# A third of the transposes of the normalised input, by the matrix engine in place of the DMA

## The chip, the cores and the metric

The kernel runs on one core of a Trainium2 chip. The metric is the device time of one execution in microseconds; the figure used is the median over several runs. The core's engines each run their own instruction stream in order: TensorE (PE, matrix products; its weight loads are shown apart as PEld), VectorE (DVE), ScalarE (ACT, called the activation engine in some places), GpSimd (POOL) and SyncE (SP), which in this kernel issues most of the DMA transfers. Streams wait for one another by semaphores.

## The reference, cut to what matters

A decoder block on x of 2048 rows by 1024 channels, in float32. Only the first stage concerns the change: x is normalised by row and multiplied by a wide input matrix; the first two blocks of columns of the product feed a recurrent branch, the rest feeds attention and gates.

```python
def rmsnorm(x, g):
    y = xf * lax.rsqrt(jnp.mean(xf * xf, axis=-1, keepdims=True) + NORM_EPS)
    return (y * g.astype(jnp.float32)).astype(x.dtype)
...
    u = rmsnorm(h, pre_g[l])
    z = jnp.einsum('bsd,df->bsf', u, w_in[l])
    xr, zr, q, k, v, za, gm = jnp.split(z, split_points, axis=-1)
    xc = causal_depthwise_conv(xr, conv_w[l], conv_b[l])
    y_r = rg_lru(xc, ...) * jax.nn.silu(zr)
...
    lam = exp(sum(attn_lq1 * attn_lk1)) - exp(sum(attn_lq2 * attn_lk2)) + lam_init
    o = diff_attention(qh, kh, vh, lam)
    m = g_r * (y_r @ w_br_rnn) + g_a * (y_a @ w_br_attn)
    h = h + rmsnorm(m @ w_out, post_g)
```

## The kernel before, in words

**The input.** x is taken in 16 tiles of 128 rows (tile i holds rows 128 i to 128 i + 127, 128 x 1024 float32). `load_x` has SP issue one transfer for a tile; five tiles are kept under way, and tile i + 5 is loaded when tile i is done with (L240). `x_stat` works on tiles in pairs: ACT squares a tile and sums each row (L256, `jk`), DVE turns the two sums into a row scale (`vx` at L257 and the small steps of an inverse square root behind it). `x_fin` then takes each tile: DVE multiplies it by the row scale and the channel gain (L266), ACT casts the product to fp16, the high half of `u16` (L269), and the rest, the low half, is the difference to that cast, made by DVE for even tiles and by POOL for odd ones (L270). Both halves are needed with channels on the partitions, so each is transposed into the tile `uT[p, hi/lo, k, s]`: channel k x 128 + p, row s. Before the change every one of these 32 transposes is a DMA that SP issues (L276):

```python
x_last[2] = la.ins
load_x(i + PD)
for hl_ in range(2):
    x_t[i] = nc.sync.dma_start_transpose(out=uT[:, hl_, :, i * 128:(i + 1) * 128],
                                         in_=u16[:, hl_])
```

**The weights.** The input matrix is used in blocks of 128 columns. A block is loaded (L145, `wst`), squared and summed by ACT (L156, `w_s` at L158), its total over the partitions taken by a 128 x 1 matmul into a PSUM tile called `tot` (L162), and it is split into a high and a low fp16 half by ACT (L177) and DVE (L178). `tot` comes from the pool `lpt`, which has two PSUM buffers.

**The first products.** A product of such a block with uT is three matmuls (high x high, high x low, low x high) for each of eight k, all at L192. The first three half rows (two `xr` blocks and a `zr` block, rows 0 to 1023) are not made one after another: their three PSUM tiles of 128 x 1024 stand open at once, and PE goes through x tiles 0 to 7, 72 matmuls of 128 x 128 for each, so that it can start on tile 0 while the later ones come. After that come the half rows of rows 1024 to 2047, in two chunks of 128 x 512 (24 matmuls each), then the further blocks.

**What follows on the other engines.** ACT reads an `xr` half row out of PSUM (L318); a four-tap convolution on POOL and DVE makes `xc`, which is split into two halves `xh` and `xl`; PE multiplies these by gate weights (L351 to L353) that DVE split before into `gwh` and `gwl` (L513, L514); ACT takes the tanh of the gates (L355, `th`). The four 64-element vectors of lambda come by DMA in `a_consts`; DVE takes two dot products (into `ld`, with `lj` as a tile for the products nobody reads), and ACT an exponential and a logarithm (L531 to L538).

**The order.** The kernel is written as one program, but the order in which it is written is not the order that runs: the framework reorders each engine's instructions at build by a simulated timeline (`TileContext(nc, schedule_with_timeline_sim=True)`). An edit in one place can therefore move instructions of other places on any engine. After the build, each engine's order is fixed.

Of the kernel before, what the change touches and what calls it, by code (L numbers as in the profile page):

```python
# [9 lines left out]
F32 = mybir.dt.float32  # L10
F32R = mybir.dt.float32r
F16 = mybir.dt.float16
# [3 lines left out]
ALU = mybir.AluOpType  # L16
# [11 lines left out]
EPS = 1e-6  # L28
GM_T = 8   # groups of gate projections kept for the end of the attention
LAG = 2    # units between a unit's scores and its product with v  # L30
ACC0 = 8.0  # projection groups ahead of the attention units
PD = 5     # x tiles loaded ahead
# order in an attention unit: scores (0, 1), exponentials (e), combination of the unit before (c),
# product with v of an earlier one (p), with projection groups between them (f: one, F: all that are due)
ORD = "0fc1eFp"
SEG_A = 2  # where a head's gate projections stand between its chunks
SEG_B = 5
# [11 lines left out]
def kernel(  # L49
# [44 lines left out]
    with ExitStack():  # L94
        ones = cst.tile([128, 128], F32, name="ones")
        nc.vector.memset(ones, 1.0)
        ones16 = cst.tile([128, 128], BF16, name="ones16")
        nc.vector.memset(ones16, 1.0)

        def tl(n, name):  # L100
# [27 lines left out]

# [1 line left out]
        class W:  # L130
            pass

        def w16_at(i):
            """one of the four places for a block of weights"""
            return lambda w: w16_p.tile([128, 2, KD, 128], F16, tag=f"w{i % 4}", name="w16")
# [24 lines left out]
        def w_scale(w, ps, fac, keep=None):  # L160
            """power of two that brings the block's norm close to 2^13 (a rough sum is enough for it)"""
            nc.tensor.matmul(ps[:, 0:1], ones16, w.ss, start=True, stop=True)  # L162
            tot = tl(1, "w_tot")
            nc.vector.tensor_scalar(out=tot, in0=ps[:, 0:1], scalar1=1e-30, scalar2=None, op0=ALU.max)
            w.sg, w.iv = keep or (tl(1, f"w_sg_{w.tag}"), tl(1, f"w_iv_{w.tag}"))
            pow2_bits(w.sg, tot, 13)
            pow2_inv(w.iv, w.sg)
            if keep is None:
                w.cz = wn_p.tile([128, 1], F32, tag=f"w_cz_{w.tag}", name="w_cz",
                                 bufs={"wg": 4, "agm": 3}.get(w.tag, 2))  # L170
                nc.vector.scalar_tensor_tensor(out=w.cz, in0=w.iv, scalar=fac, in1=cu, op0=ALU.mult, op1=ALU.mult)
# [9 lines left out]

# [1 line left out]
        utx = ExitStack()  # L183
# [3 lines left out]
        def mm3(ps, w, c0, n):  # L187
            """ps[f128, n] += w^T u over all of d, s in [c0, c0 + n)"""
            i = 0
            for k in range(KD):  # L190
                for a, b in ((0, 0), (0, 1), (1, 0)):
                    nc.tensor.matmul(ps, w.t[:, a, k, :], uT[:, b, k, c0:c0 + n],  # L192
                                     start=(i == 0), stop=(i == 3 * KD - 1))
                    i += 1

        # ================= RG-LRU branch =================
        with ExitStack() as lx:
# [21 lines left out]
            def prep_g(gr):  # L219
                """power of two that keeps the scaled, normalised input in fp16's range"""  # L220
                ss, tot = tl(1, "g_ss"), tl(1, "w_tot")
                jk = le.tile([KD, 128], F32, tag="idt", bufs=1, name="jg")
                nc.scalar.activation(jk, gr, AF.Square, accum_out=ss[0:KD])
                ps = lpt.tile([128, 1], F32, tag="tot", name="tot")
                nc.tensor.matmul(ps[:, 0:1], ones[0:KD, :], ss[0:KD], start=True, stop=True)
                nc.vector.tensor_scalar(out=tot, in0=ps[:, 0:1], scalar1=1e-30, scalar2=None, op0=ALU.max)
                pow2_bits(gi, tot, 10)
                pow2_inv(cu, gi)
# [34 lines left out]
            def x_fin(i0, n, gb):  # L263
                for i in range(i0, i0 + n):
# [10 lines left out]
                    for hl_ in range(2):  # L275
                        x_t[i] = nc.sync.dma_start_transpose(out=uT[:, hl_, :, i * 128:(i + 1) * 128],  # L276
                                                             in_=u16[:, hl_]).ins

            # weight pipeline
            order = [(C_XR if i % 2 == 0 else C_ZR) + (i // 2) * 128 for i in range(2 * KD)]  # L280
# [16 lines left out]
            def in_half(b, hf, z, w):  # L297
                """PSUM tile of a half row of an x_r (z = 0) or z_r (z = 1) block"""
                if hf == 0 and 2 * b + z < 3:
# [142 lines left out]
            x_fin(4, 2, gb)  # L442
            # per-channel vectors: rows of 128 channels, turned into columns
            rows = le.tile([65, 128], F32, tag="rows", bufs=1, name="rows")
# [24 lines left out]
            with tc.issue_after(x_last[1]):  # L469
                # block-diagonal gate weights, exact f32r hi/lo  # L470
                gf_t = []
# [13 lines left out]
            with after_x():  # L485
                nc.vector.tensor_scalar(out=ba, in0=ba, scalar1=0.5, scalar2=None, op0=ALU.mult)
                nc.vector.tensor_scalar(out=bx, in0=bx, scalar1=0.5, scalar2=None, op0=ALU.mult)
                # softplus(-a) = max(-a, 0) + log1p(exp(-|a|)), log1p(t) = 2 atanh(t / (2 + t))
                spm, spe, sps, spq, spr = (lc.tile([128, KD], F32, name=f"sp{i}") for i in range(5))
# [27 lines left out]
            def a_consts():  # L517
                with after_x():
# [7 lines left out]
                    ld = cst.tile([128, 2], F32, name="ld")  # L526
                    lj = cst.tile([128, 64], F32, name="lj")
                    for i in range(2):
                        nc.vector.tensor_tensor_reduce(out=lj, in0=lv[:, 2 * i, :], in1=lv[:, 2 * i + 1, :], op0=ALU.mult,
                                                       op1=ALU.add, scale=1.0, scalar=0.0, accum_out=ld[:, i:i + 1])  # L530
# [44 lines left out]

        # ================= differential attention and merge gates =================
        QT = S // 128
        wfac_a = cst.tile([128, KD], F32, name="wfac_a")
        ya_ss = cst.tile([128, NH * NC], F32, name="ya_ss")
        with ExitStack() as ax:  # L580
# [14 lines left out]

# [1 line left out]
            wl = {k: ws[2 * KD + i] for i, k in enumerate(ahead)}  # L597
# [16 lines left out]
            def wadv(n):  # L614
                """weight blocks up to index n ready; two more on their way"""
                while wpos[0] < min(n + 3, len(worder)) or wpos[1] < min(n + 2, len(worder)) or wpos[2] < min(n + 1, len(worder)):
# [38 lines left out]

# [1 line left out]
            Kt, Qt, Vt, Gt = {}, {}, {}, {}  # L657
# [133 lines left out]

# [1 line left out]
            class U:  # L793
# [179 lines left out]

        # ================= branch projections, merge, output projection =================
        with ExitStack() as bx_:
# [178 lines left out]

            # norm of the attention branch's rows, for a bound on the merged sum
            ya_n = bs.tile([128, 1], F32, name="ya_n")
# [52 lines left out]
```

## Time and profile before

| what | value |
|---|---|
| runs | 2505.09, 2502.2, 2505.01 us; median 2505.01 |
| profiled execution | 2506.1 us from its first to its last instruction, 1.1 above the median |
| PE busy | 2353.1 us, 94% |
| DVE busy | 1548.4 us, 62% |
| ACT busy | 1224.6 us, 49% |
| POOL busy | 679.7 us, 27% |
| DMA | 268.73 MB, 107 GB/s in the mean |

The profile is of one execution, in microseconds from the start of its span; the span is its own time. Line numbers (L192) are those of the kernel before. Names such as `ps<-uT,w` give the output and inputs of an instruction by the program's tiles. A number behind "x" is a count. Idle time is put down to the event that ended it, the releaser: "[6.43 <-ACT xr L318]" means that the engine stood still for 6.43 us, until ACT had done its instruction of line 318 that writes `xr`.

### The profile page before, as it was taken

Reading aid. Unit: us, or ns where it says so; the run is one execution under the profiler, and the core shown is the slowest. Engines: PE = TensorE matmul, PEld = TensorE weight load, DVE = VectorE, ACT = ScalarE, POOL = GpSimd, SP = SyncE. Lnnn points to the kernel's source line nnn. Section 1 sums busy time; section 2 is a strip of 40 time slices with the busy share of each in tenths; the row PEclk is TensorE's granted clock in tenths of the full one; section 3 lists DMA queues with packets and bytes.
Section 4 is the critical chain, followed back from the end, with each engine's and each line's share of the span. In section 5 each row is a group of like instructions: output and inputs, shape, how many; then the busy total and the mean of one; then the engine's idle time right before and its main releaser. Section 6 shows DMA issues by size and latency. Waiting matters only on the chain. (4 is left out here: it accounts for less than half of the span.)

```text
span 2506.1 us, 41430 instructions
## 1 busy us (share of the span) xinstructions
PE 2353.1 (94%) x15240; PEld 1355.3 (54%) x15240; DVE 1548.4 (62%) x4316; ACT 1224.6 (49%) x2156; POOL 679.7 (27%) x415
## 2 busy tenths in 40 slices
PE   6789999999998999998998999999999899999998
PEld 5344444465665665665665655655655444444443
DVE  8877667668658566667567478468467244633323
ACT  5555545456547546556456457356456244312211
POOL 3443334212222212222222222223123133322211
PEclk9899999999999999999999999999999999999999
DMA  9511111235444534635535445445445854743202
GB/s 244 104 43 48 46 42 34 76 81 119 108 96 111 113 84 108 127 82 113 115 84 114 103 96 118 95 90 124 95 90 115 251 177 135 239 148 118 84 17 101
DMA packets 541323, 268.73 MB, mean 107 GB/s; under 512 B 370504, under 2 KB 518016, under 8 KB 541120
## 3 DMA queue, kind: packets, MB, share of 16 engines
q1 hardware_dynamic: 538144, 256.74, 42.6%
q0 software_dynamic: 2816, 9.08, 1.2%
q8 instruction: 119, 1.95, 0.3%
q14 instruction: 84, 0.69, 0.1%
q10 hardware_dynamic: 160, 0.27, 0.0%
HBM read 110.79 MB, written 41.94 MB: 61 GB/s over the span
## 5 line engine op out<-in xcount | busy, mean ns | idle before, releaser
L192 PEld LDWEIGHTS <-w 128*128 128x128 f16 x5040 | 475.9, 100 | 576.5 <-issue 89.2
L192 PE MATMUL mm<-uT,w 128*128 128x512 f16 x3072 | 705.1, 383 | 12.9 <-ACT gm L728 8.9
L877 POOL TENSOR_TENSOR e<-e,e 128x1024 f16<-128x1024 f32 (+2 forms) x192 | 317.0, 1666 | 970.6 <-ACT e L876 487.0
L851 ACT ACTIVATE e<-e,nb,sc_h 128x1024 f32<-128x1024 f32 (+7 forms) x384 | 376.1, 980 | 160.8 <-DVE nb L845 125.6
L826 DVE TENSOR_SCALAR_CACHE_REDUCE e<-sc 128x1024 f32<-128x1024 f32 (+7 forms) x352 | 305.2, 880 | 134.9 <-PE sc L814 122.3
L192 PE MATMUL ps<-uT,w 128*128 128x512 f16 (+1 forms) x1968 | 354.4, 345 | 26.1 <-ACT xr L318 17.7
L711 PE MATMUL mm<-wva,uT 128*128 128x256 f16 x3072 | 352.7, 275 | 3.3 <-DVE st L668 2.6
L1094 PE MATMUL psb<-yt,w 128*128 128x512 f16 x1536 | 332.9, 379 | 2.0 <-ACT w L177 1.5
L711 PEld LDWEIGHTS <-uT 128*128 128x128 f16 x3072 | 301.5, 99 | 48.8 <-issue 2.9
L814 PE MATMUL sc<-K,Q 128*128 128x512 f16 (+3 forms) x1280 | 287.2, 351 | 19.9 <-DVE e L826 13.8
L897 PE MATMUL o<-V,pt 128*128 128x128 f16 x3264 | 224.5, 222 | 38.4 <-DMA pt<-e 38.1
L1094 PEld LDWEIGHTS <-w 128*128 128x128 f16 x1536 | 149.1, 98 | 184.9 <-issue 3.9
L897 PEld LDWEIGHTS <-pt 128*128 128x128 f16 x3264 | 200.0, 99 | 72.8 <-DMA pt<-e 46.5
L876 ACT ACTIVATE e<-e 128x1024 f16<-128x1024 f32 (+2 forms) x192 | 150.1, 802 | 143.1 <-DVE e L874 118.5
L814 PEld LDWEIGHTS <-Q 128*128 128x128 f16 x1280 | 119.6, 99 | 133.2 <-issue 20.2
L874 DVE SCALAR_TENSOR_TENSOR e<-e,rs,e 128x1024 f32<-128x1024 f32 (+2 forms) x192 | 190.0, 1017 | 2.2
L1125 PE MATMUL psf<-wo,m 128*128 128x512 f16 x720 | 155.7, 379 | 0.0
L156 ACT ACTIVATE jk<-wst 128x1024 bf16<-128x1024 f32 x80 | 84.2, 1052 | 138.7 <-DMA wst<-in_w_in_dram 102.6
L1125 PEld LDWEIGHTS <-m 128*128 128x128 f16 x768 | 75.1, 98 | 90.6
L1098 DVE SCALAR_TENSOR_TENSOR t<-gt,psb 128x512 f32<-128x512 f32 x64 | 43.8, 686 | 120.2 <-PE psb L1094 100.1
L1148 ACT ACTIVATE jk<-psf 128x1024 bf16<-128x1024 f32 x15 | 15.4, 1024 | 134.0 <-PE psf L1125 69.4
L717 DVE SCALAR_TENSOR_TENSOR V<-mm,V 128x256 f16<-128x256 f32 x64 | 26.9, 421 | 85.7 <-ACT V L716 85.6
(247 smaller groups left out, 2417.3 us busy)
## 6 DMA issues: line engine op xcount, KB each, us to landing
wst<-in_w_in_dram SPq DMA_DIRECT2D x64, 512.0 KB, 4.5
xt<-in_x_dram SPq DMA_DIRECT2D x32, 512.0 KB, 4.5
gm_d<-gm SPq DMA_DIRECT2D x64, 256.0 KB, 2.7
gt<-gm_d SPq DMA_DIRECT2D x32, 512.0 KB, 3.8
K<-st SPq DMA_DIRECT2D x128, 64.0 KB, 2.0
Q<-st SPq DMA_DIRECT2D x64, 128.0 KB, 2.4
Q<-st SPq DMA_DIRECT2D x128, 64.0 KB, 2.1
ya_d<-yT SPq DMA_DIRECT2D x64, 128.0 KB, 2.0
```

The source lines that it names most:

```text
L156: nc.scalar.activation(jk, w.st, AF.Square, accum_out=ss)
L192: nc.tensor.matmul(ps, w.t[:, a, k, :], uT[:, b, k, c0:c0 + n], start=(i == 0), stop=(i == 3 * KD - 1))
L711: nc.tensor.matmul(ps[:, j, :], uT[:, a, k, s0:s0 + 128], wt[:, b, k].rearrange("p t f -> p (t f)"), start=(i == 0), stop=(i == 3 * KD - 1))
L814: nc.tensor.matmul(ps[:, x * 128:x * 128 + m], Qt[h, t // 4][:, v, ci, q0:q0 + 128], K[:, ci, 0:m], start=(v == 0), stop=(v == 1))
L826: nc.vector.tensor_scalar(out=ev[:, 0:m], in0=ps[:, 0:m], scalar1=1.0, scalar2=None, op0=ALU.mult, op1=ALU.max, accum_out=u.mx[:, ci, col: ...
L851: nc.scalar.activation(ev[:, 0:nb * 128], ev[:, 0:nb * 128], AF.Exp, bias=nb_[:, ci:ci + 1], scale=sc_h[h], accum_out=u.sm[:, pi, ci:ci + 1])
L874: nc.vector.scalar_tensor_tensor(out=e0[:, 0:m], in0=e1v[:, 0:m], scalar=rs, in1=e0[:, 0:m], op0=ALU.mult, op1=ALU.add)
L876: nc.scalar.activation(e1[:, 0, 0:m], e0[:, 0:m], AF.Copy)
L877: nc.gpsimd.tensor_tensor(out=e1[:, 1, 0:m], in0=e0[:, 0:m], in1=e1[:, 0, 0:m], op=ALU.subtract)
L897: nc.tensor.matmul(o, pt[:, a, kb % 8, :], V[:, kb % 4, b, :], start=(kb == 0 and i == 0), stop=(kb == n - 1 and i == 2))
L1094: nc.tensor.matmul(ps, w.t[:, p, k, :], y_t[b][:, q, k, sl], start=(i == 0), stop=(i == 3 * KD - 1))
L1125: nc.tensor.matmul(pn[n], m16[:, a, j, ms], wo[:, b, j, ns], start=(j == 0 and a == 0 and b == 0), stop=(j == KD - 1 and a == 1))
```

## The change

For the x tiles with i % 3 == 2 (2, 5, 8, 11 and 14) a half is transposed by eight matmuls with an identity matrix `idh` into a PSUM tile `xps` (128 x 8 x 128 fp16), and ACT copies `xps` into uT. `xps` comes from `lpt` and shares the two buffers of the `tot` tiles. The other eleven tiles go by DMA as before. `idh` is built once at the start. To make room for it in SBUF the tile `lj` goes: the dot products of lambda now write their unread products over one of their own inputs. Line numbers of the changed kernel are 2 higher than before up to `x_fin`, and 7 or 8 higher behind it.

```diff
         ones16 = cst.tile([128, 128], BF16, name="ones16")
         nc.vector.memset(ones16, 1.0)
+        idh = cst.tile([128, 128], F16, name="idh")
+        make_identity(nc, idh)
...
                     load_x(i + PD)
                     for hl_ in range(2):
-                        x_t[i] = nc.sync.dma_start_transpose(out=uT[:, hl_, :, i * 128:(i + 1) * 128],
-                                                             in_=u16[:, hl_]).ins
+                        if i % 3 == 2:
+                            pt = lpt.tile([128, KD, 128], F16, tag="tot", name="xps")
+                            for k in range(KD):
+                                nc.tensor.transpose(pt[:, k, :], u16[:, hl_, k * 128:(k + 1) * 128], idh)
+                            nc.scalar.activation(uT[:, hl_, :, i * 128:(i + 1) * 128], pt, AF.Copy)
+                        else:
+                            x_t[i] = nc.sync.dma_start_transpose(out=uT[:, hl_, :, i * 128:(i + 1) * 128],
+                                                                 in_=u16[:, hl_]).ins
...
-                    lj = cst.tile([128, 64], F32, name="lj")
                     for i in range(2):
-                        nc.vector.tensor_tensor_reduce(out=lj, in0=lv[:, 2 * i, :], in1=lv[:, 2 * i + 1, :], op0=ALU.mult,
+                        nc.vector.tensor_tensor_reduce(out=lv[:, 2 * i, :], in0=lv[:, 2 * i, :], in1=lv[:, 2 * i + 1, :], op0=ALU.mult,
```

The reordering moves instructions beside those that the diff names. In the rows below, a row is an instruction in its engine's order: line, operation, output<-inputs with their shape; the number behind a tile's name tells its buffers apart and differs between the two builds.

The first place is SP's queue at the end of the loads of x. Before, `u16_419` is tile 9, `u16_484` tile 10 and `u16_492` tile 11; `xt_422` is the load of tile 14 and `xt_487` that of tile 15:

```order
L240 DMA xt_422<-in_x_dram 128x1024
L276 DMA_TRANSPOSE uT_82<-u16_419 128x8x128
L145 DMA wst_1231<-in_w_in_dram 128x8x128
L276 DMA_TRANSPOSE uT_82<-u16_484 128x8x128
L276 DMA_TRANSPOSE uT_82<-u16_492 128x8x128
L240 DMA xt_487<-in_x_dram 128x1024
L276 DMA_TRANSPOSE uT_82<-u16_484 128x8x128
L276 DMA_TRANSPOSE uT_82<-u16_492 128x8x128
```

Now `u16_478` is tile 9, `u16_543` tile 10, and `xt_455`, `xt_481` and `xt_546` are the loads of tiles 13, 14 and 15:

```order
L284 DMA_TRANSPOSE uT_87<-u16_478 128x8x128
L242 DMA xt_455<-in_x_dram 128x1024
L242 DMA xt_481<-in_x_dram 128x1024
L284 DMA_TRANSPOSE uT_87<-u16_478 128x8x128
L284 DMA_TRANSPOSE uT_87<-u16_543 128x8x128
L242 DMA xt_546<-in_x_dram 128x1024
L284 DMA_TRANSPOSE uT_87<-u16_543 128x8x128
L147 DMA wst_1326<-in_w_in_dram 128x8x128
```

The load of tile 15 stood behind both halves of tile 9, a weight block, and one half each of tiles 10 and 11; now it stands behind tile 9 and one half of tile 10, and the weight block comes after it.

The second place is ACT around the first read-out of `xr`. Before, `jk_535` is the square of tile 14 and `jk_537` that of tile 15; `xr_1193` is the first read-out, `u16_521` and `u16_527` are the casts of tiles 12 and 13:

```order
L269 ACTIVATE u16_484<-xt_330 128x1024
L269 ACTIVATE u16_492<-xt_373 128x1024
L256 ACTIVATE jk_535,ssx_532<-xt_422 128x1024
L318 ACTIVATE xr_1193<-ps_614,w_cz_180 128x1024
L386 ACTIVATE g_1209<-ps_615,w_cz_229 128x1024
L269 ACTIVATE u16_521<-xt_381 128x1024
L318 ACTIVATE xr_1212<-ps_616,w_cz_313 128x1024
L269 ACTIVATE u16_527<-xt_414 128x1024
L256 ACTIVATE jk_537,ssx_532<-xt_487 128x1024
```

Now `jk_612` and `jk_614` are the squares of tiles 14 and 15, `xps_554` and `xps_564` the two halves of tile 11, and `u16_598` is the cast of tile 12:

```order
L271 ACTIVATE u16_543<-xt_353 128x1024
L271 ACTIVATE u16_551<-xt_414 128x1024
L258 ACTIVATE jk_612,ssx_609<-xt_481 128x1024
L179 ACTIVATE w16_502<-wst_426,w_sg_wg_494 128x1024
L282 ACTIVATE uT_87<-xps_554 128x8x128
L258 ACTIVATE jk_614,ssx_609<-xt_546 128x1024
L326 ACTIVATE xr_1288<-ps_709,w_cz_185 128x1024
L158 ACTIVATE jk_1322,w_ss_1321<-wst_1302 128x1024
L271 ACTIVATE u16_598<-xt_422 128x1024
L282 ACTIVATE uT_87<-xps_564 128x8x128
```

The square of tile 15 stood five places behind the first `xr` and now stands straight ahead of it, with the split of a weight block and the copy of the high half of tile 11.

The third place is ACT after the first gate products; `xr_1334` before and `xr_1429` now are the same read-out, the second half row of block 0:

```order
L355 ACTIVATE th_1349<-ps_1342,prm_448 128x1024
L355 ACTIVATE th_1358<-ps_1351,prm_448 128x1024
L531 ACTIVATE ld_1760<-ld_1760 128x2
L536 ACTIVATE lsp_1768<-nlam_1765 128x1
L538 ACT_TABLE_LOAD
L538 ACTIVATE lsp_1768<-lsp_1768 128x1
L359 ACT_TABLE_LOAD
L359 ACTIVATE a_1360<-th_1349,Cn_603 128x1024
L318 ACTIVATE xr_1334<-ps_1285,w_cz_180 128x1024
```

Now, with the two copies of tile 14 at the head (`xps_636`, `xps_646`):

```order
L282 ACTIVATE uT_87<-xps_636 128x8x128
L282 ACTIVATE uT_87<-xps_646 128x8x128
L538 ACTIVATE ld_1855<-ld_1855 128x2
L543 ACTIVATE lsp_1862<-nlam_1859 128x1
L545 ACT_TABLE_LOAD
L545 ACTIVATE lsp_1862<-lsp_1862 128x1
L326 ACTIVATE xr_1429<-ps_1380,w_cz_185 128x1024
L179 ACTIVATE w16_1503<-wst_1302,w_sg_wg_1495 128x1024
L363 ACT_TABLE_LOAD
L363 ACTIVATE th_1444<-ps_1437,prm_507 128x1024
L363 ACTIVATE th_1453<-ps_1446,prm_507 128x1024
```

Both tanh stood ahead of the lambda constants and of `xr`; now they stand behind `xr` and a weight split.

On PE the 16 transposes of tile 2 stand around the products of tiles 0 and 1, those of tile 5 inside those of tiles 3 and 4, those of tile 8 in tile 5, those of tile 11 in tiles 6 and 7, and those of tile 14 in one run between the first and the second chunk of the second half row of block 0, ahead of the gate products. On POOL the low half of tile 15 and the transfers of the lambda vectors come ahead of the first `xl`. The order also differs by a few places in two heads of the attention and at the start of the branch projections.

## The prediction

> **What bounds the kernel now.** I read the page from the top: busy shares first, then the same by slices.
>
> ```profile
> PE 2353.1 (94%) x15240; PEld 1355.3 (54%) x15240; DVE 1548.4 (62%) x4316; ACT 1224.6 (49%) x2156; POOL 679.7 (27%) x415
> PE   6789999999998999998998999999999899999998
> ```
>
> TensorE (PE) is busy 94% of the span and sets the time nearly everywhere; the exception is the opening. Slices are 62.7 us long: in the first PE is at 6 tenths, in the second at 7. All that the change edits lies in the first 102 us, so its worth is the time by which the opening ends earlier, as long as a PE that is full afterwards carries that to the end. The windows view, cut where PE stops and starts, shows what is to be had (columns: window, length, busy of PE, PEld, DVE, ACT, POOL with counts, granted clock, DMA share, GB/s):
>
> ```profile
> 20.00:34.85 14.85, 9.97 (x100) 9.54 (x100) 14.61 (x39) 9.19 (x12) 4.26 (x2) 0.89 1.08 240
> 34.85:64.69 29.84, 28.77 (x479) 28.53 (x479) 24.69 (x60) 15.14 (x24) 14.45 (x17) 0.94 1.11 229
> 64.69:71.12 6.43, 0.00 (x0) 0.00 (x0) 6.05 (x14) 3.08 (x5) 2.21 (x1) 0.88 1.15 277
> 71.12:97.35 26.23, 18.33 (x74) 7.83 (x74) 25.92 (x40) 10.84 (x15) 14.19 (x8) 0.83 0.67 128
> 97.35:114.15 16.80, 12.40 (x48) 7.60 (x49) 11.63 (x49) 7.59 (x10) 5.52 (x6) 0.91 0.30 23
> 114.15:141.93 27.78, 25.44 (x111) 12.13 (x111) 25.26 (x19) 17.95 (x19) 13.35 (x6) 0.94 0.13 38
> 141.93:363.00 221.07, 209.56 (x937) 101.16 (x937) 157.21 (x193) 120.40 (x113) 81.25 (x45) 0.97 0.14 46
> ```
>
> Between 20 and 114 PE idles 4.9 + 1.1 + 6.4 + 7.9 + 4.4 = 24.7 us. Up to 71 the DMA engines are over-full (1.08 to 1.15); from 71.12 to 97.35 it is VectorE (DVE) that has no idle time (25.92 of 26.23). So two limits follow each other, DMA and then DVE. The waits of the first 130 us, and of DVE from 20 to 71, name them (total, times, longest):
>
> ```profile
> ACT jk L256 <- DMA xt<-in_x_dram: 17.1, 11, 3.4
> DVE vx L257 <- ACT jk L256: 3.3, 3, 1.4
> ```
>
> Why x comes late is seen on SP's queue: the issues of x tiles up to 130 us, with the median us from issue to landing at the row's end, and then the queue in order of time (start, duration of the issue; L240 loads an x tile, L276 transposes):
>
> ```profile
> xt<-in_x_dram SPq DMA_DIRECT2D x16, 512.0 KB, 4.7
> ```
>
> ```profile
> 37.54 0.53 SPq L240 DMA_DIRECT2D xt<-in_x_dram  x1
> 38.12 5.29 SPq L276 DMA_TRANSPOSE uT<-u  x2
> 43.50 0.53 SPq L240 DMA_DIRECT2D xt<-in_x_dram  x1
> 44.09 4.38 SPq L276 DMA_TRANSPOSE uT<-u  x2
> 48.56 0.53 SPq L240 DMA_DIRECT2D xt<-in_x_dram  x1
> ...
> 71.30 0.53 SPq L240 DMA_DIRECT2D xt<-in_x_dram  x1
> 71.88 25.88 SPq L276 DMA_TRANSPOSE uT<-u  x10
> ```
>
> A load leaves every 5 to 6 us, and 4.4 to 5.3 us of that are the two transposes queued ahead of it. The rest of the story is the timeline of the restarts of PE (start, duration, in brackets the idle time before and its releaser):
>
> ```profile
> 34.85 12.73 PE L192 MATMUL ps<-uT,w 128*128 128x128 f16 x196 [2.22 <-DMA uT<-u]
> ...
> 68.92 1.06 ACT L256 ACTIVATE jk<-xt 128x1024 bf16<-128x1024 f32 x1 [3.35 <-DMA xt<-in_x_dram]
> 69.97 1.09 ACT L318 ACTIVATE xr<-ps,w_cz 128x1024 f32<-128x1024 f32 x1
> 71.12 18.30 PE L192 MATMUL ps<-uT,w 128*128 128x512 f16 x72 [6.43 <-ACT xr L318]
> ...
> 96.47 0.74 DVE L513 CAST gwh<-gf 128x1024 fp32r<-128x1024 f32 x1
> 97.35 0.77 PE L351 MATMUL ps<-xh,gwh 128*128 128x512 f32 x1 [7.91 <-DVE gwh L513]
> ...
> 98.13 2.44 DVE L514 TENSOR_TENSOR gwl<-gf,gwh 128x1024 fp32r<-128x1024 f32 x2
> ...
> 101.09 2.12 ACT L355 ACTIVATE th<-ps,prm 128x1024 f32<-128x1024 f32 x2 [9.25 <-PE ps L353]
> 107.61 0.20 ACT L531 ACTIVATE ld<-ld 128x2 f32<-128x2 f32 x1 [4.40 <-DVE ld L529]
> ...
> 109.75 0.20 ACT L538 ACTIVATE lsp<-lsp 128x1 f32<-128x1 f32 x1
> 110.56 1.28 ACT L359 ACT_TABLE_LOAD   x1 [0.61 <-DVE xr L319]
> 111.86 1.24 ACT L359 ACTIVATE a<-th,Cn 128x1024 f32<-128x1024 f32 x1
> 113.01 1.09 ACT L318 ACTIVATE xr<-ps,w_cz 128x1024 f32<-128x1024 f32 x1
> 114.00 1.14 ACT L177 ACTIVATE w<-wst,w_sg_wg 128x1024 f16<-128x1024 f32 x1
> 114.15 22.46 PE L192 MATMUL ps<-uT,w 128*128 128x512 f16 x96 [4.39 <-ACT xr L318]
> ...
> 134.41 1.27 DVE L178 SCALAR_TENSOR_TENSOR w<-wst,w_sg_wg,w 128x1024 f16<-128x1024 f32 x1
> ...
> 141.12 0.16 PE L162 MATMUL tot<-w_s,ones 128*128 128x1 bf16 x1 [1.69 <-DVE w_s L158]
> 141.93 20.88 PE L192 MATMUL ps<-uT,w 128*128 128x512 f16 x96 [0.65 <-ACT xr L318]
> ```
>
> ScalarE (ACT) takes its work in order: the square of tile 14 waits 3.35 us for its x, the first xr stands behind it, and PE waits for that xr.
>
> **The change, part by part.** Tiles 2, 5, 8, 11 and 14 lose 10 of 32 DMA transposes and gain 80 matmuls and 10 copies. Prices:
>
> ```profile
> 52.63 12.06 PE L192 MATMUL ps<-uT,w 128*128 128x128 f16 x213
> L192 PE MATMUL ps<-uT,w 128*128 128x128 f16 x576 | 39.0, 237 | 8.4 <-DMA uT<-u 7.9 <-ACT w L177 0.5
> q1 hardware_dynamic: 5478, 1.35, 97.6%
> ```
>
> The last row is the queue from 76 to 84 us, where only transposes run: 1.35 MB at 97.6% of 8 us. One transpose moves 128 x 1024 x 2 bytes = 0.262 MB, so it costs 7.8 / 5.15 = 1.5 us of all 16 engines, and ten are 15 us of a resource that is full until 71.
>
> *A, x earlier: -2.8 us.* Each pair of transposes that goes takes 4.4 to 5.3 us out of SP's queue, ahead of later x loads, so late in the opening, with two or three pairs gone, a load is held by its buffer and no longer by the queue, and leaves some 9 us earlier. What then ends is the wait that DVE has for x, 3.3 us in three pieces; ACT's longer wait of 17.1 us is mostly cover, since DVE was still busy. From the 3.3 I take 0.5 off, because a cast of x now stands behind a copy of 1.1 us in two or three places. Bounds: nothing, and all of DVE's idle time from 34.85 to 71.12, 5.15 + 0.38 = 5.5. What is late next is DVE itself, so no more than that can come.
>
> *From 71 to 97: 0.* The same DVE instructions stand there before and after (two tanh products, six conv taps, tiles 14 and 15, the gate weights), and DVE has 0.3 us idle. The lead of A passes through. PE stands still for 7.9 us of it and hides the transposes of tile 14 as long as both halves of its input are there before the gate weights. That POOL now subtracts tile 15 before it makes the first xl is moved cover as well: the first gate matmuls need xh alone.
>
> *C, the order after the gate weights: -2.0.* ACT before does two tanh, the lambda constants, a table load, an exponential and then xr of the next block; PE waits 4.39 us for that xr. The scheduler now puts xr straight behind the lambda constants, and both tanh after it. From the cast of gwh at 96.47, PE's restart came 17.7 us later. Now: 4.1 us to the end of both gwl, 2.3 from the lambda's exponential (107.61) to the end of the logarithm (109.95), then xr 1.1, a weight cast 1.1, a table load 1.3 and two tanh 2.1, since the matmuls that follow need the second tanh's PSUM buffer: 12.0. Not in these rows, and put at 3.7 (an estimate, some eighteen steps of about 0.2 us each): DVE's cast of xh, the two dot products and the small steps between. Together 15.7, which is -2.0; bounds: the whole wait, -4.4, and +1 if the constants' DMA is late, since xr is now behind them for sure.
>
> *D, the wait at 141: -2.0.* There PE waits 1.69 and 0.65 us for the statistics of a weight block whose load was late, because DVE reached the low half of an older block only at 134.4. That step and the cast before it now come some 10 us sooner in both orders. Bounds -2.3 and 0.
>
> *E, what is added: +0.9.* On PE 80 transposes. The row with 213 matmuls of the same 128 x 128 shape spaces them 56.6 ns, so 4.5 us in all; in duration one is 237 ns, so 19.0 if they do not overlap. I take the spacing, since they stand in runs of 8 or 16 with weight loads of their own like those of that row. Of them 64 lie before PE's stop at 64.69, which has 6.4 us of slack, and the last 16 (0.9 us) can fall on the path. On ACT 10 copies at 1.1 = 11 us, nearest row the xr eviction of 128 x 1024 from PSUM (1.09) (a half-size element could make it cheaper, a slower PSUM read dearer: 0.7 to 1.5 us); ACT is busy 27.4 of 51.1 us from 20 to 71, so they fit, and the two of tile 14 run while DVE is late. Bounds 0 and +5. The identity on POOL and the lambda products in place stand at nothing: POOL is busy 4.26 of 14.85 us from 20 to 34.85, and the identity is two small instructions ahead of that.
>
> Sum: -2.8 - 2.0 - 2.0 + 0.9 = -5.9 us. Against the profiled execution's span of 2506.1 that is 2500.2. The runs' median, 2505.01, is 1.1 us below that span; so 2499.1, forecast 2499.
>
> Further on the order also moves in two heads of the attention and at the start of the branch projections, one or two places each way. PE's slices there show 9 (90% or more); I put nothing for it, and 2 us to either side in the range.
>
> [...]
>
> **Rivals.** *Hidden.* The lead is made but lost again. For it: DVE is 25.26 of 27.78 busy up to 141.93, and copies of 1.1 us on ACT delay the very casts that DVE waits for, so A could be 0 to 1, and C and D could turn into waits for a weight load. Against it: PE's own stops at 114 and 141 have a releaser that the new order moves forward. Time: A 0, C -1, D 0, E +0.9, so 2505.
>
> *ACT's new order makes it slower.* The square of tile 15 now stands ahead of the first xr; before, only that of tile 14 did. PE, and DVE's next step, wait for xr. Had x of tile 15 kept its issue at 71.30 (a landing takes some 4.7 us, so 76.0), square and read-out take 1.25 us and xr would begin at 77.3 rather than 69.97: +7.3, and the lead of A is gone; with C kept and D lost, 2505.0 + 7.3 - 2.0 + 0.9 = 2511. The point where it turns: x of tile 15 landing later than 68.7 costs at once, and later than about 72 undoes C and D too. Against it: that load is now queued behind seven transposes fewer (two each of tiles 2, 5 and 8, the first of tile 11), and seven at 2.4 us (half of the 4.38 to 5.29 that two took) are more than the 9 us that I expect of it: issue at 62 to 63, landing by 67.5.
>
> *Transposes that do not overlap.* If each takes its full 237 ns, the 64 early ones are 15.2 us, less the 2.2 us that PE waited for tile 2 and the 1.1 idle: PE stops at 76.6 in place of 64.7, 5.5 us past the restart at 71.12, the last 16 add 3.8, and C falls away, since PE itself is last: 2505.0 + 9.3 - 2.0 = 2512. It turns at about 0.13 us each. Against it is the spacing of 56.6 ns. [...] No row of this trace shows a transpose by PE.
>
> **How the numbers follow.** Half the spread of 2502.2 to 2505.09 and 0.2% (5.0 us) are about what this kernel's runs can tell apart. The forecast case holds 0.62; its own range is 2493 (A 5.5, C 4.4, D 2.3, E 0 make -12.2) to 2502, and with its middle at -5.9 I put 0.50 of it beyond -5.0 and 0.12 within. Hidden: 0.21, all within 0.2%. ACT's order: 0.10, and transposes without overlap: 0.07, both slower. So faster 0.50, same 0.33, slower 0.17. The range runs from 2493 to 2509, which leaves out most of the slow rivals and the far end of the fast case.
>
> **What would show it.** A: no waits of DVE's vx for the square in 20 to 71, and x tile 15 issued by 64. The first stop of PE shorter than 3 us (right), or longer with ACT's square of tile 15 as its last step (ACT's order). Transposes 55 to 110 ns apart in their runs, or over 200 (no overlap). PE at the gate weights by 95, and the next restart, before at 114.15, by 110. At the place of 141.93, PE four to eight us ahead, and the same lead at 363. I am wrong if a copy or cast on ACT is the last thing that PE or DVE waits for several times before 71, or if a lead at 142 is not there at 1900.

## The result, and the profile after

The changed kernel takes 2488.25 us (median of three, 2488.08 to 2490.47) against 2505.01 before: the ratio is 0.9944, interval 0.9926 to 0.9962. Run again beside the experiments it took 2486.78 us, ratio 0.9935 (0.9923 to 0.9947). So by these ratios it is faster by 14 to 16 us (the medians differ by 16.8) where 6 were forecast, and its time lies 5 us below the range. Of all the runs in this document three single executions, one each of three of the kernels below, took 2656.72 to 5295.9 us, far above every other one of their kernel, and medians and ratios leave them out.

The page of the changed kernel, busy shares and PE by slices (now 62.2 us each):

```profile
PE 2343.9 (94%) x15320; PEld 1349.9 (54%) x15320; DVE 1543.9 (62%) x4316; ACT 1232.4 (50%) x2166; POOL 681.5 (27%) x417
PE   5789999999999999999999998999999899999998
```

PE is busy 9.2 us less, though it does 80 transposes more, and idle 10.5 us less. The busy part fits the granted clock: its mean is 0.987 in this execution and 0.980 in that of before, where it stands at 0.5 for 104 us in all, against 68 now. The first slices, where all the edits are, hardly differ (5, 7, 8 against 6, 7, 8). The windows view of the changed kernel, cut at the same places of the program:

```profile
34.30:70.16 35.86, 29.42 (x510) 28.52 (x508) 31.73 (x76) 24.13 (x33) 17.28 (x18) 1.00 1.02 212
70.16:71.57 1.41, 0.00 (x1) 0.00 (x0) 1.41 (x2) 1.41 (x4) 0.00 (x0) 1.00 0.25 68
71.57:97.11 25.54, 17.39 (x91) 7.96 (x90) 25.40 (x39) 12.30 (x16) 13.52 (x11) 0.92 0.48 84
97.11:112.17 15.06, 14.18 (x49) 7.46 (x49) 13.51 (x49) 7.45 (x9) 4.51 (x2) 0.79 0.04 10
112.17:139.79 27.62, 23.95 (x112) 11.67 (x111) 16.13 (x24) 18.88 (x19) 11.80 (x5) 1.00 0.12 34
139.79:361.80 222.01, 207.86 (x938) 100.76 (x938) 162.72 (x190) 119.78 (x113) 83.92 (x46) 0.98 0.14 46
```

PE's stop of 6.43 us has shrunk to 1.41, yet PE starts again at 71.57, where it was 71.12. At 139.79 PE is 2.1 us ahead, and 222 us later only 1.2. The rest must lie behind that. Both traces have equally many matmuls of each output, apart from the transposes, so the k-th of one can be set beside the k-th of the other. Start before less start after, median over 50 us from the time given (time of before):

```
time   150   200   350   500   800   850   950  1150  1350  1500  1800  1900  2000  2050
lead  0.24  0.10  1.17  2.99  1.73  4.93  7.11  8.36 11.79  9.73 15.19 15.27 17.25 19.74
```

(These two executions differ by 19.7 us; the timed runs by 14 to 16.) One trace of a kernel can drift by as much as half of this: the kernel before with 256 instructions added, which below takes the same time as before, leads the trace of before by 9.5 us at 1900, at a granted clock of 0.983. So the table only shows where to look; what a step is worth has to come from the timed runs, or from steps that return in many traces. The lead grows in steps, most of them in the attention between 800 and 1860 us, hundreds of microseconds behind the last line that the diff touches, and one at the start of the branch projections near 2000.

### The profile page after: what moved, and what is told of

It reads as the page before. It is cut to its first block, busy times and chain, and to the rows that moved or that the text cites. A ratio compares the mean times of both kernels' runs of the same rounds, so it can differ in the third digit from the quotient of the medians.

```text
span 2486.4 us, 41574 instructions
## 1 busy us (share of the span) xinstructions
PE 2343.9 (94%) x15320; PEld 1349.9 (54%) x15320; DVE 1543.9 (62%) x4316; ACT 1232.4 (50%) x2166; POOL 681.5 (27%) x417
## 5 line engine op out<-in xcount | busy, mean ns | idle before, releaser
L194 PE MATMUL mm<-uT,w 128*128 128x512 f16 x3072 | 704.1, 382 | 10.7 <-ACT gm L735 7.0
L194 PE MATMUL ps<-uT,w 128*128 128x512 f16 (+1 forms) x1968 | 348.5, 340 | 18.1 <-ACT xr L326 8.9
L904 PE MATMUL o<-V,pt 128*128 128x128 f16 x3264 | 220.6, 219 | 29.5 <-DMA pt<-e 29.1
L904 PEld LDWEIGHTS <-pt 128*128 128x128 f16 x3264 | 196.0, 98 | 64.5 <-DMA pt<-e 38.1
L837 DVE CUSTOM_DVE_ANT_0 e<-sc,mask 128x128 f32<-128x128 f32 x256 | 72.7, 285 | 10.6 <-PE sc L821 8.9
```

The source lines that it names most:

```text
L904: nc.tensor.matmul(o, pt[:, a, kb % 8, :], V[:, kb % 4, b, :], start=(kb == 0 and i == 0), stop=(kb == n - 1 and i == 2))
```

## Where the steps of the attention are

One of the steps, first before and then after: PE waits for a block `pt` of attention weights, which a DMA transposes.

```profile
854.86 2.53 PE L897 MATMUL o<-V,pt 128*128 128x128 f16 x22 [2.52 <-DMA pt<-e]
```

```profile
851.45 1.40 PE L904 MATMUL o<-V,pt 128*128 128x128 f16 x22 [0.84 <-DMA pt<-e]
```

Ahead of this place both kernels have the same instructions in the same order for 650 us. Before, the wait is 1.7 us longer, and the 22 matmuls behind it take 1.1 us longer: the windows view gives a granted clock of 0.50 over them before and of 1.00 after. The DMA view over the flight of that transpose (850 to 855 us before; 848.2 to 851.5 after; packets, MB, share; the last row ends with the median from issue to landing, of one landing on record before):

```profile
q1 hardware_dynamic: 1499, 0.58, 47.9%
q8 instruction: 1, 0.02, 1.1%
...
pt<-e SPq DMA_TRANSPOSE x2, 4.8
```

```profile
q1 hardware_dynamic: 1357, 0.33, 51.0%
...
pt<-e SPq DMA_TRANSPOSE x2, 2.7
```

Before, one packet of queue 8 falls into the flight: a packet of instructions, 16,384 bytes, which holds one of the 16 DMA engines for 0.88 us (1.1% of 16 engines' 5 us). The transpose lands 4.80 us after its issue, and after the change, without such a packet, 3.13. Over the whole trace of before, queue 8 brings 119 such packets of 1.08 us on average, one for every 256 of PE's 30,480 matmuls and weight loads; from one packet to the next PE starts 255 of these in the median, and 254 after the change. So the packets go with PE's count and are taken as its code. Of the attention's 384 transposes 333 have a landing on record. 59 of them took over 3.9 us, and in 44 of these flights (from 1.2 us behind the issue to 0.3 ahead of the landing) an instruction packet of queue 8 or 14 was under way. 254 took up to 3.4 us, and 21 of these met one. Setting the two kernels side by side is sharper: 76 transposes take over 0.8 us longer in one of them than in the other, and by the same measure the slower of the two met a packet of queue 8 in 65 of these pairs, the faster in none.

That gives a theory: instructions added at the start shift every later packet against the program. The changed kernel has 160 instructions more on PE (80 transposes and their weight loads), so each packet comes at a place of the program 160 instructions earlier, and other transposes are hit. In the two traces the k-th packet of queue 8 does start at the same count of PE's instructions (after less before: 2 in the median, -32 to 43 in nine of ten). A rival, that PE itself stops for its code, is out: between 363 and 1900 us the idle time of PE that ends with nothing but its own issue is 1.2 us or less in each of the fifteen traces that can be read.

## The experiments

Ratios are to the kernel before, on the same chip. "Position" is the number of instructions that PE has more than before, taken modulo 256.

| kernel | position | rows moved behind the opening | median us | ratio (interval) |
|---|---|---|---|---|
| identity and lambda products alone | 0 | none | 2503.21 | 0.9999 (0.9990 to 1.0009) |
| before, 256 added | 0 | none | 2502.99 | 1.0005 (0.9994 to 1.0015) |
| tiles 2 and 5, 192 added | 0 | none | 2502.09 | 0.9997 (0.9988 to 1.0007) |
| tiles 5 and 8, 192 added | 0 | attention | 2501.49 | 0.9985 (0.9974 to 0.9996) |
| tiles 8 and 11, 192 added | 0 | branch start | 2498.67 | 0.9982 (0.9972 to 0.9991) |
| changed, 96 added | 0 | both | 2497.11 | 0.9971 (0.9960 to 0.9982) |
| before, 64 added | 64 | none | 2495.25 | 0.9967 (0.9955 to 0.9979) |
| tiles 2 and 5 | 64 | none | 2494.30 | 0.9961 (0.9948 to 0.9974) |
| tiles 5 and 8 | 64 | attention | 2499.37 | 0.9980 (0.9971 to 0.9990) |
| tiles 8 and 11 | 64 | branch start | 2493.11 | 0.9955 (0.9943 to 0.9967) |
| changed, 160 added | 64 | both | 2491.77 | 0.9953 (0.9940 to 0.9966) |
| before, 160 added | 160 | none | 2498.95 | 0.9980 (0.9967 to 0.9992) |
| changed, again | 160 | both | 2486.78 | 0.9935 (0.9923 to 0.9947) |
| changed, 32 added | 192 | both | 2491.49 | 0.9948 (0.9934 to 0.9961) |
| changed, 64 added | 224 | both | 2493.78 | 0.9957 (0.9943 to 0.9970) |

**Fewer tiles.** Four kernels (the identity alone, and tiles 2 and 5, 8 and 11, or 5 and 8 with nothing added) differ from the changed one in the tiles that PE transposes, which also changes what the scheduler moves:

```diff
-                        if i % 3 == 2:
+                        if i < 0:          # identity alone; the others: i in (2, 5), (8, 11), (5, 8)
```

> All 32 transposes by DMA, but with the identity tile, its two POOL instructions and the lambda products in place as in the changed kernel. The order of every engine is that of before, apart from the identity on POOL. Theory Order (the gain behind the opening comes from the rows that the scheduler moved in two heads of the attention and at the start of the branch projections): no gain, 2505 within 3 us. Theory Layout (it comes from tiles and code that now lie elsewhere in memory, which changes how long single transposes by DMA take to land and where they meet the matmuls): a good part of the 7 us that the attention gained ahead of its first moved rows shows here too, 2498. Theory Phase (every small shift of the opening deals the landings of the attention's transposes anew): 2505 within 3 us, since the opening doesn't shift.

> Tiles 2 and 5 alone by the matrix engine. The scheduler moves rows of the opening, and none behind it. Theory Order: what the opening brings, 0 to 2 us, so 2503 to 2505, with the lead at 1900 us that of 363. Theory Layout: 2498 as in the kernel with the identity alone. Theory Phase: the lead changes by several us between 363 and 1900, to either side, so 2495 to 2510 with no relation to the lead at 363.

> Tiles 8 and 11 alone by the matrix engine. Behind the opening the scheduler moves rows at the start of the branch projections alone, the same ones as in the changed kernel. Theory Order: the opening's 0 to 2 us and the 4.4 us between 1972 and 2030, so about 2499, with the lead at 1900 that of 363. Theory Layout: 7 us more, 2493. Theory Phase: a lead at 1900 unlike that at 363, and in any case a step of 4 to 5 us between 1972 and 2030.

> Tiles 5 and 8 alone by the matrix engine. Behind the opening the scheduler moves rows in two heads of the attention alone, the same ones as in the changed kernel. Theory Order: the opening's 0 to 2 us and some 3 us between 1160 and 1235 and at 1590, so about 2501, with no step between 1972 and 2030. Theory Layout: 7 us more, 2494. Theory Phase: steps at other places of the attention too.

The identity alone gave nothing, so theory Layout is out, and its transposes land as before: only 7 of 333 differ by over 0.8 us. Tiles 2 and 5 brought 9.8 us (0.0039 of 2503.8) with no row moved behind the opening and with a lead of -1.1 at 350 us: theory Order is out as the whole answer, and so is a lead carried from the opening. Phase expected no relation between kernels, and that is wrong too: the three partial changes share their late landings (5 to 21 of 340 differ), though their openings and moved rows differ. What they have in common is four DMA transposes fewer, or 64 instructions more on PE.

**Instructions alone.** So the next kernels add instructions to PE and change nothing else; every engine's order stays the same apart from them. They are matmuls of one column, which nobody reads, while PE is idle ahead of 12 us (half of them ahead of the first weight block where there are more than 48):

```diff
                 ps = lpt.tile([128, 1], F32, tag="tot", name="tot")
+                for _ in range(N):
+                    nc.tensor.matmul(ps[:, 0:1], ones16, ones16[:, 0:1], start=True, stop=True)
                 nc.tensor.matmul(ps[:, 0:1], ones[0:KD, :], ss[0:KD], start=True, stop=True)
```

> The kernel before, all transposes by DMA, with 80 matmuls of a single column into an unread PSUM column, in PE's idle time ahead of 12 us. With their weight loads they are 160 instructions more for PE, as many as the 80 transposes of the change bring; every engine's order is otherwise that of before. Theory Code position (PE's code comes in packets of 16 KB, one for every 256 instructions, and a transpose of the attention that meets such a packet on a DMA engine lands some 1.3 us late; so instructions added at the start deal the late landings anew): the late transposes are the same ones as in the changed kernel, and the attention gains about as there without moved rows, 5 to 10 us, so 2495 to 2500. Theory Queue position (what counts is how many transposes went through the queue before): late landings as before, 2504. The opening gains nothing in either.

> The kernel before with 32 such matmuls: 64 instructions more for PE, as many as two tiles transposed by PE bring. Theory Code position: the late landings are those of the kernels with tiles 2 and 5, 5 and 8, or 8 and 11 by PE, and the time is near theirs, 2494 to 2499. Theory Queue position: 2504, late landings as before.

> The kernel before with 128 such matmuls: 256 instructions, one whole packet of code. Theory Code position: the packets fall on the same places of the program as before, late landings as before, and 2504 within 2 us. This also shows whether the added matmuls as such cost or bring something. Theory Queue position: 2504 as well.

> The changed kernel with 48 such matmuls: 160 + 96 = 256 instructions more for PE than before, so that the packets of code fall on the same places of the program as before. Theory Code position: late landings mostly as in the kernel before; what the attention gained ahead of its first moved rows, some 6 us, goes, and what the opening and the moved rows bring stays: 2494 to 2499. Theory Queue position: late landings as in the changed kernel, 2488.

All four came out as Code position said. 32 useless matmuls make the kernel before 8.3 us faster (0.0033 of 2504.0), 80 make it 5.0 faster, 128 (one whole packet) change nothing. 48 of them make the changed kernel 9 us slower (0.9971 against 0.9935). The changed kernel with 96 added has ten DMA transposes fewer than before and still lands them as before, so Queue position is out. At the step shown above, the kernel before with 256 added, the changed one with 96 added, and the kernel before with 160 added, in this order:

```profile
851.52 2.53 PE L902 MATMUL o<-V,pt 128*128 128x128 f16 x22 [2.60 <-DMA pt<-e]
```

```profile
855.09 1.62 PE L906 MATMUL o<-V,pt 128*128 128x128 f16 x22 [2.62 <-DMA pt<-e]
```

```profile
854.50 1.40 PE L902 MATMUL o<-V,pt 128*128 128x128 f16 x22 [0.80 <-DMA pt<-e]
```

At position 0 the transpose is late and PE waits 2.5 to 2.6 us; at 160 it waits 0.8. In all seven traces of position 0 this transpose took 4.5 to 4.9 us, in the other eight that can be read 3.1 (3.07 to 3.15). And the step in the lead between 800 and 850 us is 3.2 to 3.3 us in these eight, and -0.3 to 0.1 in the six traces of position 0 that can be set beside before. So this step, 1.73 to 4.93 in the table of leads, is shown to be one of position.

The waits view from 363 to 1900 us has the sum of such waits (total, times, longest); the kernel before, the changed kernel, and the changed kernel with 96 added:

```profile
PE o L897 <- DMA pt<-e: 38.1, 30, 3.2
```

```profile
PE o L904 <- DMA pt<-e: 29.1, 29, 2.5
```

```profile
PE o L906 <- DMA pt<-e: 35.9, 29, 3.8
```

Over the seven traces of position 0 the sum is 35.9 to 39.5 us. At 160 it is 28.5 to 32.4 (the kernel before with 160 added has 32.4), at 224 29.5, at 64 31.0 in the kernel before and 29.4 with tiles 2 and 5, but 35.7 with tiles 5 and 8 and 36.4 with tiles 8 and 11. So the sum falls with position in most kernels, and in these two by little: it is not the whole of the gain, and single traces do not settle how the rest divides between other waits and the granted clock. Nor are fewer transposes late at the better positions: in each of the fifteen traces 50 to 64 of those on record took over 3.9 us. Position decides which ones, and so for which PE has to wait. Transposes whose time to landing differs by over 0.8 us between two kernels, of 289 to 342 that can be set side by side:

```
both at position 0 (seven kernels)                     4 to 14
both at position 64 (four)                             5 to 21
both at position 160 (three)                           8 to 17
one at 0, 64 or 160 and the other at another of these  65 to 87
```

**The parts with the position held.** With 96 matmuls (192 instructions) added, a kernel of two tiles by PE is back at position 0. What is left is its own.

> The changed kernel once more, on the chip of the three below, since its first time rests on three runs: 2488 within 3 us.

> Tiles 2 and 5 by PE and 96 matmuls of a single column: 64 + 192 = 256 instructions more for PE than before, so the code packets stand as before. No rows moved behind the opening, so this is what the opening of a partial change brings by itself. Theory Code position: 2503 to 2505, and its gain of some 9 us without the added matmuls is gone. Rival, the lead of the opening carries: 2494 as without them.

> Tiles 8 and 11 by PE and the same 96 matmuls: code packets as before, rows moved at the start of the branch projections alone, as in the changed kernel. Theory Code position with moved rows worth 3 to 4 us there: 2500 to 2501, with a step of 3 to 4 us in the lead between 1950 and 2050. Rival, moved rows are worth nothing: 2504.

> Tiles 5 and 8 by PE and 96 matmuls of a single column: code packets as before, rows moved in two heads of the attention alone, the same ones as in the changed kernel. If those rows are worth what the two traces differ by there, some 3 us, 2501; if that difference was packets too, 2503 to 2504; if they cost something, 2505 or more.

> The changed kernel with 80 added matmuls: 320 instructions more for PE than before, which is a packet and 64. Theory Code position, with parts that add up: the 7 us that the changed kernel keeps with the packets as before (2497), and the 8.8 us that 64 added instructions brought to the kernel before: 2488 to 2489, late landings as in the kernel before with 64. If the parts don't add up, 2493 to 2495.

> The changed kernel with 16 added matmuls, 192 instructions more for PE than before. Theory Code position: the late landings are dealt anew once more, and the time is one from 2484 to 2498, the range of the positions tried so far with this program; if position were only a matter of packets as before or not, it would be 2487.

> The changed kernel with 32 added matmuls, 224 instructions more than before: as for the kernel with 16, 2484 to 2498, and by theory Code position a time of its own.

Tiles 2 and 5 then bring nothing (0.9997 against 0.9961 without the added ones). The rows moved at the start of the branch projections bring 0.0018, 4.5 us. There PE ran into the statistics and the split of the first projection weights. PE's timeline before:

```profile
1987.11 7.03 PE L192 MATMUL mm<-uT,w 128*128 128x512 f16 x24 [4.34 <-ACT gm L728]
...
1996.08 12.00 PE L1094 MATMUL psb<-yt,w 128*128 128x512 f16 x54 [1.50 <-ACT w L177]
...
2012.48 0.59 PE L1094 MATMUL psb<-yt,w 128*128 128x512 f16 x2 [0.48 <-DVE t L1098]
...
2027.03 0.16 PE L162 MATMUL tot<-w_s,ones 128*128 128x1 bf16 x1 [2.47 <-DVE w_s L158]
```

With tiles 8 and 11 by PE and 192 added, where these rows alone are moved:

```profile
1978.71 0.17 PE L164 MATMUL tot<-w_s,ones 128*128 128x1 bf16 x1
1983.73 6.89 PE L194 MATMUL mm<-uT,w 128*128 128x512 f16 x24 [4.85 <-ACT gm L740]
1990.46 0.17 PE L164 MATMUL tot<-w_s,ones 128*128 128x1 bf16 x1
1990.48 14.19 PE L1106 MATMUL psb<-yt,w 128*128 128x512 f16 x65
```

The sum of a weight block now stands ahead of the last gate projections and is done in the shadow of the wait for `gm`; the waits of 1.50, 0.48 and 2.47 us are gone. Of these the 1.50 is in all nine traces without the moved rows and in none of the six with them; the 2.47 (0.56 to 3.14 in others) is missing in three of the nine too, so it is not the moved rows alone that take it away. In the leads, the six kernels with these rows moved whose trace can be read step by 3.2 to 6.2 us between 1950 and 2050, the others by -0.4 to 2.0. The rows moved in the attention gave 0.9985 (3.8 us), which barely clears zero, and at their own place (1150 to 1200 us) the lead falls from 3.9 to 3.0: where that gain would lie is open. At position 64 the same kernel (0.9980) is if anything slower than the two without moved rows (0.9961 and 0.9967), so that these rows bring a gain of their own is not shown.

At three more positions the changed kernel took 2491.49 to 2493.78 us. For 160 added, 2488 to 2489 was expected if the parts add up and 2493 to 2495 if not; it was 2491.77, between the two, and its interval (2488.6 to 2495.1) reaches both, so whether they add up is open. For 32 added, Code position gave only a wide span and 2487 was the rival's; the interval of that time is 2488.7 to 2495.4, just above the rival's value, which is all it shows. Two of these three have no trace that can be read, so whether their late landings moved as expected is open there; with 64 added 58 to 89 differ from every other kernel. No position tried beats the one that the change happened to have, though the intervals of all three overlap with its own.

## Why the prediction was wrong, by its own steps

**The step that failed** is the end of the sum: "PE's slices there show 9 (90% or more); I put nothing for it, and 2 us to either side in the range." Behind the opening lie nearly all of the 16 us: about 9 from code position (0.9935 against 0.9971, two intervals that do not overlap) and about 4 from the moved rows at the branch start (0.9982). Some 3 are left, which the opening and the moved rows of the attention may hold and which no experiment places. A slice at 9 tenths hides waits of 38.1 us in 30 places for `pt`, in the waits view of before. And a shift of code appeared in no part, cost or rival. The clock, for which the prediction's sum has no term, does not bring the gain back into the opening: up to the place of 141.93 PE's busy time grew from 96.37 to 98.20 us, with the transposes, and only behind that place is it shorter, by 11.1 us.

**The opening** was to bring 5.9 us and brought 0.1 at 170, 1.2 at 362. From the timeline of the changed kernel:

```profile
53.37 0.62 PE L281 MATMUL xps<-idh,u 128*128 128x128 f16 x8 [3.16 <-ACT u L271]
...
69.37 1.06 ACT L258 ACTIVATE jk<-xt 128x1024 bf16<-128x1024 f32 x1 [2.26 <-DMA xt<-in_x_dram]
...
70.42 1.09 ACT L326 ACTIVATE xr<-ps,w_cz 128x1024 f32<-128x1024 f32 x1
...
71.57 15.70 PE L194 MATMUL ps<-uT,w 128*128 128x512 f16 x72 [1.41 <-ACT xr L326]
...
97.11 1.40 PE L359 MATMUL ps<-xh,gwh 128*128 128x512 f32 x2 [3.42 <-DVE gwh L521]
...
112.17 10.54 PE L194 MATMUL ps<-uT,w 128*128 128x512 f16 x48
...
124.94 10.52 PE L194 MATMUL ps<-uT,w 128*128 128x512 f16 x48 [2.23 <-ACT th L363]
135.11 0.58 PE L359 MATMUL ps<-xh,gwh 128*128 128x512 f32 x1
...
139.79 20.89 PE L194 MATMUL ps<-uT,w 128*128 128x512 f16 x96
...
166.35 0.16 PE L164 MATMUL tot<-w_s,ones 128*128 128x1 bf16 x1 [2.86 <-DVE w_s L160]
...
166.65 0.15 DVE L117 TENSOR_SCALAR ytau<-yme 128x1 int32<-128x1 int32 x1
...
169.89 0.58 PE L194 MATMUL ps<-uT,w 128*128 128x512 f16 x1 [3.37 <-ACT xr L326]
```

And those of before that answer to the last ones and were not shown yet:

```profile
136.26 0.58 PE L351 MATMUL ps<-xh,gwh 128*128 128x512 f32 x1
...
166.75 0.15 DVE L115 TENSOR_SCALAR ytau<-yme 128x1 int32<-128x1 int32 x1
...
169.99 0.59 PE L192 MATMUL ps<-uT,w 128*128 128x512 f16 x1 [3.12 <-ACT xr L318]
```

- A (-2.8): wrong, +0.45 in its place (71.12 to 71.57). The rival on ACT's new order had the mechanism: the square of tile 15 waits 2.26 us for x, and xr stands behind it. It was to cost from a landing past 68.7; tile 15 was issued at 64.99, 6.3 us sooner than before and not 9, and landed at 69.28. DVE still waits 1.8 of its 3.3 us for the squares. The rival's size (+7.3) took the old issue time, which was far off.
- 71 to 97, nothing: right, 97.35 became 97.11.
- C (-2.0): right in place and size, 114.15 became 112.17. Part of the stop came back as the 2.23 us that PE now waits for `th`, behind half of the next products.
- D (-2.0): half. Ahead of that place the lead is 1.15 (136.26 to 135.11), behind it 2.14 (141.93 to 139.79). Then it is lost: at 169.89 PE starts again where it did at 169.99. ACT's xr there stands behind the read-out of `yh`, which takes its scale `ytau` from DVE, and DVE gets to that at 166.65, 0.1 us sooner than before. So Hidden was right on the opening: the lead was made, and DVE took it back. Why DVE comes as late as before there was not tried.
- E (+0.9): the prices were right. In the groups by line up to 130 us:

```profile
L282 ACT ACTIVATE uT<-xps 128x1024 f16<-128x1024 f16 x10 | 10.0, 1008 | 4.5 <-PE xps L281 4.5
L281 PE MATMUL xps<-idh,u 128*128 128x128 f16 x80 | 6.6, 229 | 10.7 <-ACT u L271 6.4 <-DVE u L272 4.3
```

A copy takes 1.01 us (1.1 taken), and eight transposes take 0.62 us from the first start to the last end, 57 ns apart at 219 ns each: they overlap, and that rival is out. The cost that I left out stands in the second row: PE waits 10.7 us ahead of transposes for the casts and low halves they read, with the products of earlier tiles queued behind them (4.3 of it in the stop ahead of the gate weights, where PE stands anyway). Four of the five waits for a cast lie before 71, which the prediction had named as a sign of being wrong.

The forecast's sign came true, but of its reasons only C and the prices did. That the 160 instructions of the change put its code at the best of the positions tried was luck.

## What to carry to other kernels

Instructions added at the start moved the code packets here against everything behind them, and in this kernel, where DMA transposes end waits of PE (38.1 us of them before), that alone moved the time by up to 9 us of 2500. Before a gain of a few tenths of a per cent is put down to an edit, run the edit with instructions added to make up whole packets (256 here), or only as many instructions without the edit. And compare leads along the whole program, not only where the edit is: here nearly all of the difference was elsewhere. Do so with more than one trace, since two traces of kernels that take the same time differed by 9.5 us here.

## What the hardware showed

One packet of PE's code was 16,384 bytes, came once per 256 instructions (119 for 30,480), and held one DMA engine for 1.08 us on average, as long as some 50 of the transposes' own packets of 256 bytes (about 20 ns each: 1357 packets in 51.0% of 16 engines' 3.3 us). A transpose that met one landed 1.7 us later at the step shown above (4.80 us in place of 3.13). Which ones did was nearly the same from one execution to the next (8 of 342 differ between the changed kernel's two traces) and from one kernel to another, as long as PE's instruction count agreed modulo 256 (4 to 21 differ, against 65 to 87 where it did not, for positions 0, 64 and 160). At that step PE waited 1.7 us longer, and the 22 matmuls behind the wait took 2.53 us in place of 1.40, at a granted clock of 0.50 in place of 1.00. That a long wait lowers the clock is not shown: with 96 added to the changed kernel the wait was 2.62 us and the matmuls took 1.62.
